# A decoder layer on one core: the 512×4096×1024 W_down product by seven block products in place of eight

## The chip, the cores and the metric

The kernel runs on one core of a Trainium2 chip. The metric is the device time of one execution in microseconds (us); less is better. Three executions of the kernel before were timed, and one more was recorded by the hardware profiler. Five engines work side by side: PE (TensorE, matrix products; its weight loads are listed as PEld), DVE (VectorE), ACT (ScalarE), POOL (GpSimd) and SP (SyncE, which issues the DMA transfers here). Each takes its own instructions in order and waits on semaphores for the others.

## The reference

One layer for 512 tokens of width 1024, all in f32. Cut to what matters:

```
h = rms_norm(x, g_pre_mix);  proj = h @ w_in
q, k, v, cb, cc, cu, ga, gc = split(proj)
y_attn = stick_breaking_attention(q, k, v) @ w_attn_out      # 8 heads x 64
y_conv = (cb * causal_dwconv3(cc * cu)) @ w_conv_out
mixed = (sigmoid(ga) * y_attn + sigmoid(gc) * y_conv) @ w_o
x = x + rms_norm(mixed, g_post_mix)
f = relu(rms_norm(x, g_pre_mlp) @ w_up)**2 @ w_down          # 1024 -> 4096 -> 1024
x = x + rms_norm(f, g_post_mlp)
x = x + sigmoid(rms_norm(x, g_ple) @ w_ple_gate) * (p @ w_ple_proj)
```

## The kernel before

Every large product is made with three matmuls: each f32 operand is **split** into a high part (an ACT cast to the type fp32r) and a low part (a DVE subtraction of the high part from the source), and high×high, high×low and low×high are added up in PSUM (`mm3`, lines 82 to 85; `split`, lines 60 to 62). So each weight matrix is loaded as f32 into one of four `raw` buffers, cast by ACT, subtracted by DVE, and only then read by PE. Weights that come in columns (`wcols`) or rows (`wrow`) are split in two halves of 128x512; the split pair lies in `wlo` and `whi`, five buffers each.

The stages stand in this order: head (norm of x, transposes, v), attention and convolution, **mix** (line 408: for each of 8 column blocks two gate products and one product with W_attn_out and W_conv_out), **W_o** (`rows`, line 489), the small p @ W_ple_proj (line 493), **up** (lines 512 to 532: 32 column blocks of W_up, each 24 matmuls of 512 columns, followed by `relu2`, which leaves the activations in eight f32 tiles `af`, 8 KB a partition), **W_down** (line 562) and the **gate product** with W_ple_gate (line 567 on).

`rows` runs k outermost over the row blocks of a weight, for all four token blocks t and both halves of the columns, into eight PSUM banks; the last four k are kept back and run token block by token block, and after each the chain of norm, residual and next norm starts (`residual`, `chain1`, `chain2`), whose result is transposed on PE two token blocks later (`transposed2`). For W_down that is 32 row blocks × 4 token blocks × 2 column halves × 3 = 768 matmuls of 512 columns. In each chain, `rstd_of` ends with a 128x1 power on POOL (line 119); this and the masks of the attention are all that POOL computes.

PE and SP issue in the order in which the code stands (`manual_schedule`, line 35). The order on ACT, DVE and POOL is made by the framework's scheduler when the kernel is built. A buffer is given out again when the last reader of its former content is done; the writer waits for that. SP's queue is one line: a transfer that waits for its buffer holds back all the transfers behind it.

Of the kernel before, what the change touches and what calls it, by code (L numbers as in the profile page):

```python
# [8 lines left out]
F32 = mybir.dt.float32  # L9
# [14 lines left out]
FF = 4096  # L24
EPS = 1e-6
# [6 lines left out]
def hybrid_block(ctx, tc, x, p, g_pre_mix, w_in, b_gate, w_conv, w_attn_out, w_conv_out, w_o,  # L32
# [10 lines left out]
    wts = ctx.enter_context(tc.tile_pool(name="wts", bufs=5))  # L43
# [5 lines left out]
    psp = ctx.enter_context(tc.tile_pool(name="psp", bufs=8, space=bass.MemoryType.PSUM))  # L49

# [13 lines left out]
    def weights(loads, shape):  # L64
        raw = raws.tile(shape, F32, tag="raw", name="raw")
        for sel, src in loads(raw):
            nc.sync.dma_start(sel, src)
        lo = wts.tile(shape, F32R, tag="wlo", name="wlo")
        hi = wts.tile(shape, F32R, tag="whi", name="whi")
# [3 lines left out]
        return hi, lo  # L73

# [7 lines left out]
    def mm3(ps, lh, ll, rh, rl, start, stop):  # L82
        nc.tensor.matmul(ps, lh, rh, start=start, stop=False)  # L83
        nc.tensor.matmul(ps, lh, rl, start=False, stop=False)  # L84
        nc.tensor.matmul(ps, ll, rh, start=False, stop=stop)  # L85
# [322 lines left out]
    for j in range(NK):  # L408
        sa, sc = sg if j == 0 else (gate(j, 0), gate(j, 1))
# [27 lines left out]
    def rows(nk, stat, w, tail, chain):  # L437
        acc = {}
        held = {}
        for k in range(nk):  # L440
            wk = wrow(w, k)
            if k >= nk - tail:
                held[k] = wk
                continue
            sh, sl = stat(k)
            for t in range(NT):
                tok = slice(t * P, (t + 1) * P)
                for hf in range(2):
                    if k == 0:
                        acc[t, hf] = bank()  # L450
                    cs = slice(hf * 512, (hf + 1) * 512)
                    mm3(acc[t, hf], sh[:, tok], sl[:, tok], wk[0][:, cs], wk[1][:, cs], k == 0, False)
        for t in range(NT):
# [7 lines left out]
            chain(t, [acc[t, 0], acc[t, 1]])  # L461

# [52 lines left out]
    for half in range(2):  # L515
        ns = slice(half * 256, (half + 1) * 256)
        for c in range(2):
# [8 lines left out]
            if half == 1:  # L526
                relu2(c, ups[c])
    for c in range(2, FF // P):
        if c == 8:
            gpl = gain(g_post_mlp)  # L530
            gle = gain(g_ple)
        relu2(c, proj(wcols(w_up, c * P), hm))

    a_s = {}
    pgw = {}

    def acts(c):
        g = c // 4
        if g not in a_s:
            a_s[g] = (bigt([P, 4, S], name="ah"), bigt([P, 4, S], name="al"))  # L540
            for i in range(4):
                split(a_s[g][0][:, i], a_s[g][1][:, i], af[g][:, i])
            if 4 <= g < 7:
                i = g - 4
                wl = bigt([P, 2, D], name="pgl")
                wh = bigt([P, 2, D], name="pgh")
                for kk in range(2):
                    pgw[2 * i + kk] = (wh[:, kk], wl[:, kk])
                    raw = raws.tile([P, D], F32, tag="raw", name="raw")
                    nc.sync.dma_start(raw, w_pg[(2 * i + kk) * P:(2 * i + kk + 1) * P, :])  # L550
                    split(wh[:, kk], wl[:, kk], raw)
        return a_s[g][0][:, c % 4], a_s[g][1][:, c % 4]

    hn2 = {}
    h3 = hpair("h3")

    def chain2(t, accs):
        hn2[t] = residual(xr[t // 2][:, t % 2, :], accs, gpl, gle)
        if t > 1:
            transposed2(h3, hn2[t - 2], t - 2)  # L560

    rows(FF // P, acts, w_down, 4, chain2)
    for k in range(6, NK):
        pgw[k] = wrow(w_pg, k)

# [1 line left out]
    for t in range(NT):  # L567
        if t == 1:
            transposed2(h3, hn2[3], 3)
        tok = slice(t * P, (t + 1) * P)  # L570
        for cs in CUTS[t]:
            n = cs.stop - cs.start
            ps = bank()[:, 0:n]
            for k in range(NK):
                mm3(ps, h3[0][k // 4][:, k % 4, tok], h3[1][k // 4][:, k % 4, tok],
                    pgw[k][0][:, cs], pgw[k][1][:, cs], k == 0, k == NK - 1)
            if t == 0 and cs.start == 0:
                transposed2(h3, hn2[2], 2)
            sg = tm()[:, 0:n]
            nc.scalar.activation(sg, ps, AF.Sigmoid)  # L580
# [31 lines left out]
```

## Time and profile before

| | before |
|---|---|
| median of 3 timed runs (lowest to highest) | 768.4 us (766.04 to 769.82) |
| the profiled execution: first to last instruction | 764.4 us |
| median of the timed runs above that span | 4.0 us |
| W_down, first to last matmul | about 538 to 713 us of the span |
| up | about 364 to 538 us |
| gate product, to the last output | about 713 to 764 us |
| granted PE clock, mean | 1.000 |
| mean rate of all DMA transfers | 102 GB/s |

The time of the profiled execution itself is not listed beside its span, so the span is set against the median of the timed runs. A row of the groups reads: line, engine, operation, written tile <- read tiles, shape, number; then the busy time of all, the mean of one in ns, and how long the engine had stood idle before them, with what ended most of that. A row of the windows gives for each engine the busy time and the number of instructions that fall into the stretch.

### The profile page before, as it was taken

To read this page: it belongs to the slowest core of one execution; us is meant where nothing else is said; L and a number is where in the kernel's file an instruction comes from. 1 tells how busy PE (TensorE), PEld (TensorE's weight loads), DVE (VectorE), ACT (ScalarE), POOL (GpSimd) and SP (SyncE) were. 2 spreads that over 40 slices of the span, in tenths; PEclk is the share of its full clock that TensorE was granted. 3 is DMA by queue.
4 is the path that set the end of the run, shared out by engine and by line. 5 is a ranking of instruction groups with operands and counts; after the bars stand their busy time and mean duration, and the time that the engine had idled before them with its cause. 6 is when DMAs were issued, how large, how long until landed. Compare 5 with 4: busy or idle time off the path is not lost.

```text
span 764.4 us, 9131 instructions
## 1 busy us (share of the span) xinstructions
PE 756.4 (99%) x3528; PEld 631.9 (83%) x3528; DVE 388.1 (51%) x643; ACT 301.7 (39%) x586; POOL 49.8 (7%) x91
## 2 busy tenths in 40 slices
PE   8999999999999999999999999999999999999997
PEld 6888888888888888888988888888888888888886
DVE  5759797976434345348433333333652543234742
ACT  7654645554333334228323232323631433222511
POOL 1013314040000000001000000000000000000100
PEclk9999999999999999999999999999999999999999
DMA  9512130414634623211633333332323442410011
GB/s 303 163 58 83 55 111 29 131 31 115 193 111 130 200 87 106 83 56 34 187 86 108 86 107 89 104 101 94 110 84 109 138 165 87 161 56 1 0 56 55
DMA packets 91106, 77.66 MB, mean 102 GB/s; under 512 B 2580, under 2 KB 81208, under 8 KB 91064
## 3 DMA queue, kind: packets, MB, share of 16 engines
q1 hardware_dynamic: 91064, 77.10, 32.9%
q8 instruction: 27, 0.44, 0.2%
q14 instruction: 15, 0.12, 0.1%
HBM read 74.99 MB, written 2.10 MB: 101 GB/s over the span
## 4 chain that ended last, share of the span: by engine, by line
PE 98%; ACT 1%; DMA 1%; DVE 0%; issue 0%; SPq 0%; POOL 0%; ACTq 0%
PE ps L83 31%; PE ps L85 31%; PE ps L84 31%; PE ps L334 1%; PE ps L320 1%; PE ps L127 1%; PE ps L293 1%; PE ps L292 1%; DMA xin<-in_x_dram 1%; ACT h1h L197 0%; PE ps L188 0%; ACT vh L61 0%; ACT junk L111 0%; PE ps L433 0%; POOL rs L119 0%
## 5 line engine op out<-in xcount | busy, mean ns | idle before, releaser
L62 DVE TENSOR_TENSOR wlo<-raw,whi 128x512 fp32r<-128x512 f32 x236 | 158.2, 686 | 253.2 <-ACT whi L61 253.0
L61 ACT CAST whi<-raw 128x512 fp32r<-128x512 f32 x236 | 141.5, 623 | 328.1 <-PE ps L84 174.8
L83 PE MATMUL ps<-h1h,whi 128*128 128x512 f32 x288 | 113.0, 392 | 0.0
L85 PE MATMUL ps<-h1h,wlo 128*128 128x512 f32 x288 | 112.3, 390 | 0.0
L84 PE MATMUL ps<-h1l,whi 128*128 128x512 f32 x288 | 112.2, 390 | 0.0
L83 PE MATMUL ps<-h2h,whi 128*128 128x512 f32 (+1 forms) x272 | 102.5, 377 | 0.0
L84 PE MATMUL ps<-h2l,whi 128*128 128x512 f32 (+1 forms) x272 | 102.4, 377 | 0.0
L85 PE MATMUL ps<-h2h,wlo 128*128 128x512 f32 (+1 forms) x272 | 102.4, 377 | 0.0
L83 PE MATMUL ps<-whi,ah 128*128 128x512 f32 x256 | 99.7, 389 | 0.0
L85 PE MATMUL ps<-whi,al 128*128 128x512 f32 x256 | 99.6, 389 | 0.0
L84 PE MATMUL ps<-wlo,ah 128*128 128x512 f32 x256 | 99.6, 389 | 0.0
L85 PEld LDWEIGHTS ps<-h1h,wlo 128*128 128x128 f32 x288 | 54.1, 188 | 11.2
L84 PEld LDWEIGHTS ps<-h1l,whi 128*128 128x128 f32 x288 | 54.1, 188 | 10.9
L83 PEld LDWEIGHTS ps<-h1h,whi 128*128 128x128 f32 x288 | 54.1, 188 | 10.8
L85 PEld LDWEIGHTS ps<-h2h,wlo 128*128 128x128 f32 x272 | 51.2, 188 | 9.4
L84 PEld LDWEIGHTS ps<-h2l,whi 128*128 128x128 f32 x272 | 51.2, 188 | 9.4
L83 PEld LDWEIGHTS ps<-h2h,whi 128*128 128x128 f32 x272 | 51.2, 188 | 9.3
L84 PEld LDWEIGHTS ps<-wlo,ah 128*128 128x128 f32 x256 | 48.1, 188 | 10.0
L85 PEld LDWEIGHTS ps<-whi,al 128*128 128x128 f32 x256 | 48.1, 188 | 9.9
L83 PEld LDWEIGHTS ps<-whi,ah 128*128 128x128 f32 x256 | 48.1, 188 | 9.9
L119 POOL TENSOR_TENSOR rs<-ms,mhalf 128x1 f32<-128x1 f32 x20 | 11.8, 588 | 565.7 <-DVE ms L117 513.5
L301 POOL TENSOR_SCALAR_AFFINE_SELECT beta<-beta 128x128 f32<-128x128 f32 x32 | 26.3, 833 | 107.9 <-ACT beta L295 107.7
(133 smaller groups left out, 1000.3 us busy)
## 6 DMA issues: line engine op xcount, KB each, us to landing
raw<-in_w_in_dram SPq DMA_DIRECT2D x36, 512.0 KB, 3.8
raw<-in_w_up_dram SPq DMA_DIRECT2D x32, 512.0 KB, 4.0
raw<-in_w_down_dram SPq DMA_DIRECT2D x32, 512.0 KB, 3.3
raw<-in_w_o_dram SPq DMA_DIRECT2D x8, 512.0 KB, 3.4
raw<-in_w_ple_gate_dram SPq DMA_DIRECT2D x8, 512.0 KB, 3.3
xin<-in_x_dram SPq DMA_DIRECT2D x4, 512.0 KB, 9.5
vr<-in_w_in_dram SPq DMA_DIRECT2D x4, 512.0 KB, 7.5
raw<-in_w_conv_out_dram SPq DMA_DIRECT2D x8, 256.0 KB, 2.8
```

The lines of the kernel that those rows point to most:

```text
L61: nc.scalar.copy(hi, src)
L62: nc.vector.tensor_tensor(lo, src, hi.bitcast(F32), op=ALU.subtract)
L83: nc.tensor.matmul(ps, lh, rh, start=start, stop=False)
L84: nc.tensor.matmul(ps, lh, rl, start=False, stop=False)
L85: nc.tensor.matmul(ps, ll, rh, start=False, stop=stop)
L119: nc.gpsimd.tensor_tensor(r, m, mhalf, op=ALU.pow)
L127: nc.tensor.transpose(ps[:, i * P:(i + 1) * P], hn[g][:, i * P:(i + 1) * P], ident)
L292: nc.tensor.matmul(ps[:, c0:c0 + n], lhs, st[:, 1, 0:n], start=True, stop=False)
L293: nc.tensor.matmul(ps[:, c0:c0 + n], lhs, st[:, 2, 0:n], start=False, stop=True)
L301: nc.gpsimd.affine_select(t_[:, dg], t_[:, dg], pattern=[[-1, P]], compare_op=ALU.is_gt, fill=fill, base=0, channel_multiplier=1)
L320: nc.tensor.transpose(ps[:, c0 + (qb - kb) * P:c0 + (qb - kb + 1) * P], w[:, o:o + P], ident)
L334: nc.tensor.matmul(ps[:, kb * P:S], lhs, wt[i][:, c0:c0 + n], start=(kb == 0 and i == 0), stop=(kb == NT - 1 and i == 1))
```

## The change

The W_down product is cut into 2×2 blocks: the tokens into 0 to 255 and 256 to 511, the 4096 inner columns into two halves (16 row blocks of 128 each), and the 1024 output columns into two halves. Seven products of such blocks, taken of sums and differences of blocks (Strassen's method in Winograd's form), replace eight.

- **Sums of the weight** (`make_sums`, `save_sums`): for each of the 16 row blocks j of a half, SP loads the rows j of both halves (two transfers of 512 KB), POOL makes four differences of 128x512, and SP later writes them to a DRAM scratch tile (two transfers). One such step stands before the gates of mix blocks 2 to 7, one at the start and one behind W_o, and one at every third column block of up from 3 to 24. The stores stand in SP's line behind later weight loads.
- **Sums of the activations**: DVE, in place in `af`: four additions during up (behind the column blocks 19, 23, 27 and 31) and twelve subtractions of 128x4x256 during the first three products.
- **The seven products** run one after the other in the order 1, 2, 6, 7, 5, 3, 4, each as 8 weight tiles of 128x2x512 (`load_t`, from W_down or from the scratch) against 4 groups of activations of 128x4x256 (`load_s`), for two token blocks; each weight tile serves 12 matmuls. Each tile and each group is split anew for each product. At the end of a product ACT or DVE takes the two accumulators into f32 tiles `cx`; products 6, 5 and 4 go on adding into the banks of 1, 6 and 7.
- **Pools**: the ten weight buffers become one ring of 13 (`wts`), which also holds the inputs and outputs of the sums and later `cx`.
- **End**: the chains of token blocks 0 and 1 stand behind product 3 and inside product 4; the gate product takes token blocks 0 and 1 first, in two halves of k, then 2 and 3. In mix, the first gate of block 1 stands between the two halves of block 0's output products.

```diff
-    wts = ctx.enter_context(tc.tile_pool(name="wts", bufs=5))
+    wts = ctx.enter_context(tc.tile_pool(name="wts", bufs=13))
...
+    def make_sums():
+        save_sums()
+        j = next(made)
+        q = []
+        for h in range(2):
+            t = w4()
+            nc.sync.dma_start(t, wd[j][h].rearrange("p (c n) -> p c n", c=2))
+            q += [t[:, 0], t[:, 1]]
+        dst = wsum[j // 2][:, :, j % 2, :]
+        o = [w4(), w4()]
+        t1, t2, t3, t4 = (o[i // 2][:, i % 2] for i in range(4))
+        for r, x_, y_ in ((t1, q[1], q[0]), (t2, q[3], t1), (t3, q[3], q[1]), (t4, q[2], t2)):
+            nc.gpsimd.tensor_tensor(r, x_, y_, op=ALU.subtract)
+        unsaved.extend([(dst[:, 0:2], o[0]), (dst[:, 2:4], o[1])])
...
     for c in range(2, FF // P):
...
+        if c % 3 == 0 and c < 27:
+            make_sums()
+        if c % 3 == 2:
+            save_sums()
         relu2(c, proj(wcols(w_up, c * P), hm))
+        if c > 16 and c % 4 == 3:
+            g = c // 4 - 4
+            nc.vector.tensor_tensor(quarter(1, 0, g), quarter(1, 0, g), quarter(1, 1, g), op=ALU.add)
...
+    ORDER = (1, 2, 6, 7, 5, 3, 4)
...
+    def load_t(n, i):
+        raw = raws.tile([P, 2, 512], F32, tag="raw", name="raw")
...
+        nc.sync.dma_start(raw, src)
+        lo, hi = w4(F32R), w4(F32R)
+        split(hi, lo, raw)
...
+    def load_s(n, g):
...
+        split(hi, lo, quarter(*LEFT[n], g))
...
+        if n == 1:
+            nc.vector.tensor_tensor(a11, quarter(1, 0, g), a11, op=ALU.subtract)
+        elif n == 2:
+            nc.vector.tensor_tensor(a12, a12, a11, op=ALU.subtract)
+        elif n == 6:
+            nc.vector.tensor_tensor(a11, quarter(1, 1, g), a11, op=ALU.subtract)
...
-    rows(FF // P, acts, w_down, 4, chain2)
-    for k in range(6, NK):
-        pgw[k] = wrow(w_pg, k)
...
+    AFTER = {(3, 7): lambda: chain2(0), (4, 1): lambda: chain2(1), (4, 2): lambda: load_pg(0),
+             (4, 4): lambda: load_pg(2), (4, 5): lambda: turn(0)}
+    nt = ns = 0
+    for n, i in plan_t:
+        while ns < min(len(plan_s), plan_s.index((n, i // 2)) + 3):
+            load_s(*plan_s[ns])
+            ns += 1
+        while nt < min(len(plan_t), plan_t.index((n, i)) + 4):
+            load_t(*plan_t[nt])
+            nt += 1
+        for t in range(2):
...
+            for j in (2 * i, 2 * i + 1):
+                sh, sl = stat[n, j]
+                th, tl = tiles[n, j]
+                mm3(acc[n, t], sh[:, ts], sl[:, ts], th, tl, j == 0 and n in (1, 2, 7, 3),
+                    j == NJ - 1, n in (6, 5, 4))
+            if i == NI - 1:
+                done(n, t)
+        if (n, i) in AFTER:
+            AFTER[n, i]()
+    turn(1)
+    for t in range(2, NT):
+        chain2(t)
+        for k in range(2 * t, 2 * t + 2):
+            pgw[k] = wrow(w_pg, k)
...
+    top = [(t, cs, bank()) for t in range(2) for cs in CUTS[0]]
+    for half in range(2):
+        for t in range(2):
+            for k in range(4 * half, 4 * half + 4):
+                for t_, cs, ps in top[2 * t:2 * t + 2]:
+                    pg_mm(ps, t, cs, k)
+            if (half, t) == (1, 1):
+                turn(2)
...
+    turn(3)
```

What this does to the order on three engines. **POOL, in the chains behind W_o** (`rs` is the 128x1 power of a chain, two for each token block; the `w_` tiles are the inputs and outputs of one step of sums; L294 is the subtraction in `make_sums`). Before, behind the last masks of the attention (L301), all powers of these chains and of those behind W_down follow each other:

```order
L301 AFFINE_SELECT beta<-beta 128x128 x2
L301 AFFINE_SELECT keep<-keep 128x128 x2
L301 AFFINE_SELECT beta<-beta 128x128
L301 AFFINE_SELECT keep<-keep 128x128
L119 TENSOR_TENSOR rs<-ms,mhalf 128x1 x16
```

and now:

```order
L294 TENSOR_TENSOR w_3196<-w_3193,w_3195 128x512
L124 TENSOR_TENSOR rs<-ms,mhalf 128x1 x7
L294 TENSOR_TENSOR w_3465<-w_3461 128x512
L294 TENSOR_TENSOR w_3465<-w_3463,w_3465 128x512
L294 TENSOR_TENSOR w_3466<-w_3463,w_3461 128x512
L294 TENSOR_TENSOR w_3466<-w_3463,w_3465 128x512
L124 TENSOR_TENSOR rs<-ms,mhalf 128x1
```

One whole step of sums stands between the seventh and the eighth power, that is inside the chain of token block 3.

**DVE, where up ends and W_down begins.** Before (L510 is `relu2`, `al` the low part of an activation, `wlo` of a weight):

```order
L510 SCALAR_TENSOR_TENSOR af<-ps,tmp 128x512
L62 TENSOR_TENSOR wlo<-raw,whi 128x512
L62 TENSOR_TENSOR al<-af,ah 128x512 x7
L62 TENSOR_TENSOR wlo<-raw,whi 128x512 x2
L62 TENSOR_TENSOR al<-af,ah 128x512
```

and now, from the low parts of the second and third group of product 1 on (`sb`; they take buffers that are free only when up's last matmul is done). L632 and L593 are sums of activations, L560 is `relu2` of the last column block, `w_4662`, `w_4684` and `w_4702` are the low parts of the weight tiles 4, 5 and 6 of product 1:

```order
L64 TENSOR_TENSOR sb<-af,sb 128x1024 x2
L632 TENSOR_TENSOR af<-af 128x4x256
L560 SCALAR_TENSOR_TENSOR af<-ps,tmp 128x512
L632 TENSOR_TENSOR af<-af 128x4x256
L593 TENSOR_TENSOR af<-af 128x4x256
L64 TENSOR_TENSOR w_4662<-raw,w_4663 128x1024
L64 TENSOR_TENSOR sb<-af,sb 128x1024
L64 TENSOR_TENSOR w_4684<-raw,w_4685 128x1024
L632 TENSOR_TENSOR af<-af 128x4x256
L64 TENSOR_TENSOR w_4702<-raw,w_4703 128x1024
```

Between the weight tiles stand the splits of the groups and the sums of activations.

**SP, in up.** Before, the weights of the column blocks follow each other, with two gain vectors (`gb`) behind the eighth:

```order
L67 DMA raw<-in_w_o_dram 128x1024 x8
L67 DMA raw<-in_w_up_dram 128x8x128 x8
L104 DMA gb<-in_g_post_mlp_dram 128x1024
L104 DMA gb<-in_g_ple_dram 128x1024
L67 DMA raw<-in_w_up_dram 128x8x128 x24
```

and now, for three column blocks (L288 loads the inputs of one step of sums, L278 stores its outputs):

```order
L288 DMA w_3705<-in_w_down_dram 128x1024
L288 DMA w_3707<-in_w_down_dram 128x1024
L69 DMA raw<-in_w_up_dram 128x8x128 x2
L278 DMA wsum_415<-w_3709 128x2x512
L278 DMA wsum_415<-w_3710 128x2x512
L69 DMA raw<-in_w_up_dram 128x8x128
```

Every third weight load stands behind two stores that wait for POOL.

More of the change, by code (lines that the diff above doesn't have):

```diff
@@ L263, in hybrid_block, with save_sums @@
     hx = mov(h1)
+    wd = w_down.rearrange("(h j p) n -> j h p n", h=2, p=P)
+    wsum = [sums.tile([P, 4, 2, 512], F32, name=f"wsum{i}") for i in range(NJ // 2)]
+    unsaved = []
+    def save_sums():
+        while unsaved:
+            dst, src = unsaved.pop(0)
+            nc.sync.dma_start(dst, src)
+    made = iter(range(NJ))
+    def make_sums():
[12 more added lines that the diff above has]
+        unsaved.extend([(dst[:, 0:2], o[0]), (dst[:, 2:4], o[1])])
     def proj_q(j):
@@ L531, in hybrid_block @@
             gle = gain(g_ple)
+        if c % 3 == 0 and c < 27:
+            make_sums()
+        if c % 3 == 2:
+            save_sums()
         relu2(c, proj(wcols(w_up, c * P), hm))
-    a_s = {}
-    pgw = {}
[L537 to L552, printed above, removed]
@@ new lines, in load_s @@
+    def load_s(n, g):
+        if (n, g) == (1, 0):
+            hi, lo = (wts.tile([P, 4, 256], F32R, tag="w", name="s0") for _ in range(2))
+        else:
+            both = bigt([P, 2, 4, 256], name="sb")
+            hi, lo = both[:, 0], both[:, 1]
+        split(hi, lo, quarter(*LEFT[n], g))
+        for v in range(4):
+            stat[n, 4 * g + v] = hi[:, v], lo[:, v]
+        a11, a12 = quarter(0, 0, g), quarter(0, 1, g)
+        if n == 1:
[4 more added lines that the diff above has]
+            nc.vector.tensor_tensor(a11, quarter(1, 1, g), a11, op=ALU.subtract)
@@ new lines, in hybrid_block, with load_pg, turn @@
+    pgw = {}
+    def load_pg(k):
+        wl, wh = bigt([P, 2, D], name="pgl"), bigt([P, 2, D], name="pgh")
+        for kk in range(2):
+            pgw[k + kk] = (wh[:, kk], wl[:, kk])
+            raw = raws.tile([P, D], F32, tag="raw", name="raw")
+            nc.sync.dma_start(raw, w_pg[(k + kk) * P:(k + kk + 1) * P, :])
+            split(wh[:, kk], wl[:, kk], raw)
+    def turn(t):
+        if not h3:
+            h3.extend(hpair("h3"))
+        transposed2(h3, hn2[t], t)
+    plan_t = [(n, i) for n in ORDER for i in range(NI)]
@@ new lines, in hybrid_block @@
+    top = [(t, cs, bank()) for t in range(2) for cs in CUTS[0]]
[6 more added lines that the diff above has]
+                turn(2)
+            if (half, t) == (1, 0):
+                for args in top[:2]:
+                    gated(*args)
+    turn(3)
+    for args in top[2:]:
+        gated(*args)
@@ L571, in hybrid_block @@
+    for t in range(2, NT):
         for cs in CUTS[t]:
-            n = cs.stop - cs.start
-            ps = bank()[:, 0:n]
+            ps = bank()[:, 0:cs.stop - cs.start]
             for k in range(NK):
[L575 to L580, printed above, removed]
```

103 lines of the change are left out of this document (83 added, 20 removed).

## The prediction

> **What bounds the kernel now.** I read the page first, then the waits of PE, then PE's instructions in order of time within W_down.
>
> ```profile
> span 764.4 us, 9131 instructions
> PE 756.4 (99%) x3528; PEld 631.9 (83%) x3528; DVE 388.1 (51%) x643; ACT 301.7 (39%) x586; POOL 49.8 (7%) x91
> PE 98%; ACT 1%; DMA 1%; DVE 0%; issue 0%; SPq 0%; POOL 0%; ACTq 0%
> ...
> PE ps L169 <- POOL ident masks.py:199: 1.4, 1, 1.4
> PE ps L84 <- DVE vl L62: 1.0, 1, 1.0
> PE ps L83 <- ACT vh L61: 1.0, 1, 1.0
> PE ps L188 <- DVE xin L178: 0.2, 1, 0.2
> ```
>
> A busy PE is not yet PE at its peak, but here three views agree: PE is busy 99% of the span, the chain that ended last is PE for 98%, and PE waited for others 3.6 us in all (line, releaser, total us, times, longest), every bit of it in the head. So time falls only where PE issues less, and rises only where something new makes PE wait. The question is how fast the stream of matmuls is.
>
> ```profile
> 544.81 0.39 PE L84 MATMUL ps<-wlo,ah 128*128 128x512 f32 x1
> ...
> 548.89 0.39 PE L84 MATMUL ps<-wlo,ah 128*128 128x512 f32 x1
> ```
>
> These are the first and the last of 19 matmuls in a row, start and modelled length first: 18 steps in 4.08 us, so **0.2267 us** each. The 0.39 us is latency, not the price.
>
> **What is removed.** W_down has 32 row blocks × 4 token blocks × 2 halves × 3 = 768 matmuls of 512 columns. Seven products have 7 × 16 row blocks × 2 token blocks × 3 = 672, of the same shape. 96 × 0.2267 = **21.8 us** less on PE. All other stages keep their matmuls. This is the whole gain; the rest of the working asks what PE must now wait for.
>
> **W_down on DVE and ACT.** The new splits are 56 weight tiles and 28 groups, each 1024 wide, and 12 sums of activations of that size.
>
> ```profile
> L62 DVE TENSOR_TENSOR pgl<-raw,pgh 128x1024 fp32r<-128x1024 f32 x6 | 7.3, 1224 | 19.6 <-ACT pgh L61 16.3 <-PE ps L84 3.3
> L61 ACT CAST pgh<-raw 128x1024 fp32r<-128x1024 f32 x6 | 6.3, 1050 | 18.4 <-DMA raw<-in_w_ple_gate_dram 18.4
> L510 DVE SCALAR_TENSOR_TENSOR af<-ps,tmp 128x512 f32<-128x512 f32 x32 | 21.8, 683 | 0.0
> 538.00:713.00 175.00, 175.00 (x778) 145.04 (x777) 72.97 (x115) 62.44 (x113) 2.75 (x5) 1.00 0.30 97
> ```
>
> The last row is the window of W_down: its length, then busy time of PE, PEld, DVE, ACT and POOL, the granted clock, the DMA share and GB/s. DVE was busy 73 of 175 us. Now a group of activations lasts PE 24 matmuls, 5.44 us, in which DVE makes two weight tiles, one group and, in products 1, 2 and 6, one sum: 4 × 1.224 = 4.90 us, or 90%. In the other four products it is 3 × 1.224 = 3.67 us. ACT needs 3 × 1.05 = 3.15 us. Both fit, and the f32 sums, which the trace doesn't show, are taken at 1.224 as the nearest row of that size; at half of it DVE has 80%, at 1.5 times it 101%, which would cost PE 12 × 0.08 us, about 1 us. The buffers let DVE run three to four weight tiles ahead, 8 to 11 us.
>
> The tightest place is the seam. Groups two and three of product 1 need buffers that up holds to its last matmul. Counted from there, the DVE rows shown with the change make tile 4 after one cast and six steps of 1.224 and one of 0.683: 1.05 + 7.34 + 0.68 = 9.1 us. PE reaches tile 4 after four tiles of 12 matmuls, 10.9 us. Tile 5 is ready at 11.5 (wanted at 13.6), tile 6 at 14.0 (16.3). It fits by 1.8 us: cost **0**, with up to 3 us if hand-overs take more.
>
> **The sums on POOL.** Sixteen steps of four subtractions 128x512, two inputs each.
>
> ```profile
> L301 POOL TENSOR_SCALAR_AFFINE_SELECT beta<-beta 128x128 f32<-128x128 f32 x32 | 26.3, 833 | 107.9 <-ACT beta L295 107.7
> L301 POOL TENSOR_SCALAR_AFFINE_SELECT keep<-keep 128x128 f32<-128x128 f32 x32 | 12.6, 404 | 0.8 <-ACT keep L296 0.8
> L119 POOL TENSOR_TENSOR rs<-ms,mhalf 128x1 f32<-128x1 f32 x20 | 11.8, 588 | 565.7 <-DVE ms L117 513.5 <-DVE ms L115 52.2
> raw<-in_w_up_dram SPq DMA_DIRECT2D x32, 512.0 KB, 4.0
> 184.00:305.00 121.00, 121.00 (x540) 100.29 (x539) 52.17 (x77) 40.51 (x69) 0.00 (x0) 1.00 0.43 135
> 364.00:538.00 174.00, 174.00 (x814) 146.04 (x814) 62.98 (x101) 53.91 (x100) 0.00 (x0) 1.00 0.35 106
> ```
>
> No such operation is in the trace. From below it costs 0.59 us (the 128x1 power), from above 4 × 0.833 = 3.3 us. I take 4 × 0.404 = **1.6 us**, from the mask that doesn't wait for another engine. A step then takes 6.4 us, and one comes every three column blocks, 3 × 24 × 0.2267 = 16.3 us. POOL was idle in mix and up (the two windows, mix first), and DVE busy 43% and 36% of them, so POOL's work stands beside PE's. A step's second input waits until PE has left the column block five before; the two weight loads behind it are thus 5 × 5.44 = 27 us early, and the third stands behind POOL and its own 4.0 us of landing and is still some 20 us early (38 less 4 less 6.4 less 4 less the split). In SP's line nothing reaches PE late: cost 0. New traffic is 1 MB in and 1 MB out in 16.3 us, 129 GB/s on top of the windows' 106 to 135, and about 193 GB/s in W_down (512 KB for 12 matmuls); the head's first slice moved 303, so I count nothing.
>
> [...]
>
> ```profile
> 355.52 0.93 POOL L119 TENSOR_TENSOR rs<-ms,mhalf 128x1 f32<-128x1 f32 x1 [2.19 <-DVE ms L117]
> 361.03 0.55 POOL L119 TENSOR_TENSOR rs<-ms,mhalf 128x1 f32<-128x1 f32 x1 [4.58 <-DVE ms L115]
> 361.62 1.41 DVE L475 SCALAR_TENSOR_TENSOR tmp<-xr,rs,gb 128x512 f32<-128x512 f32 x2
> 365.73 1.04 PE L127 MATMUL ps<-ident,tmp 128*128 128x128 f32 x8
> L469 DVE TENSOR_TENSOR xr<-xr,tmp 128x512 f32<-128x512 f32 x16 | 10.3, 683 | 0.0
> ```
>
> Only here does a step stand in a chain that PE waits for: between the seventh and the eighth power behind W_o. Its inputs wait for W_o's last matmuls and land before 355. It would run from 356.5 to 356.5 + 6.4 = 362.9, so the eighth power is 1.9 us late; two residual additions that may change places with it add 1.4. PE wants the result 2.7 us after it was ready (363.0 against 365.7). So 3.3 − 2.7 = **0.6 us**; nothing at 0.59 us a subtraction, 7 us at 3.3.
>
> **The end.** In product 4 (21.8 us and 0.9 us of transposes) DVE has to make five weight tiles and four gate tiles (9 × 1.224 = 11.0), two whole chains (each two 128x1024 products and an addition, twice the 128x512 rows: 1.41 + 1.37 + 1.41 = 4.2) and two or three small steps (2 us): 21.4 of 22.7 us until PE transposes token block 1. I charge **1 us** for a fit that close. Chains 2 and 3 lie under the 96 matmuls of the upper token blocks. The last transposes are followed at once by the matmuls that need them; before, 1.74 us of two such rounds had other matmuls behind them. Two sigmoids, a cast and a subtraction must pass:
>
> ```profile
> L580 ACT ACTIVATE tmp<-ps 128x512 f32<-128x512 f32 (+1 forms) x9 | 5.0, 552 | 29.9 <-PE ps L85 29.9
> L61 ACT CAST h3h<-ps 128x512 fp32r<-128x512 f32 x8 | 4.4, 588 | 0.0
> L62 DVE TENSOR_TENSOR h3l<-ps,h3h 128x512 fp32r<-128x512 f32 x8 | 5.4, 682 | 0.0
> ```
>
> 2 × 0.55 + 0.59 + 0.68 = 2.4 us, less 1.74: **0.7 us**. The first gate of mix block 1, put between two products, gains nothing, as PE didn't wait there.
>
> **Sum.** 764.4 − 21.8 + 0.6 + 1.0 + 0.7 = 744.9 us of span. The timed runs' median of 768.4 lies 4.0 above the span; kept, that gives **748.9 us**. With all bounds at their good ends it is 746.6, with all at their bad ends (1 + 3 at the seam, 7, 3 and 2 at the end) 762.6.
>
> **Rivals.**
> - *DVE runs dry in W_down.* For it: 90% of three products, 21.4 of 22.7 us at the end, and every tile needs a cast first. Against it: four products at 67% and a lead of 8 to 11 us. If each of the 96 steps of 1024 cost 0.1 us more in hand-overs, products 1, 2 and 6 would miss their pace by nothing (5.3 of 5.44) but the seam and the end would lose about 1 and 3 us; at 0.3 us more the twelve groups with sums lose 0.66 us each, 8 us, and the two places 4 to 6: some **760 us**.
> - *POOL sets the pace of mix and up*, through SP's line: the next inputs stand behind the stores, the stores behind POOL. A round is 4.0 us of landing and four subtractions; it outlasts PE's 16.3 us from 3.1 us a subtraction on. With 14 rounds and 27 us of lead, the saving is gone at 4 × T = 12.3 + (27 + 21.8) / 14, T = 3.95 us. [...] For it: no such row in the trace. Against it: 4 × 0.404.
> - *The saving doesn't show*: the many tiles, each with its own waits, slow the stream. At 672 matmuls 0.032 us more for each eats the 21.8 us: **768 us**. Against it: every weight of before brings PE a wait for its high and its low part too, and PE's 3.6 us of waiting all lie in the head.
>
> [...]
>
> **Chances.** Forecast 0.68, DVE dry 0.17, POOL's pace 0.06, no saving shown 0.05, something else 0.04, a quarter of it slower than before. The range of 8 in 10 reaches from the best sum, less the spread of the timed runs (about 2 us), into the first rival: **744.8 to 760**. Within 0.5% of 768.4, about what a measurement of this kernel can tell from no change, lie 764.6 to 772.2: faster 0.88, the same 0.05, slower 0.07.
>
> **What would show it.** Right: 672 matmuls in W_down at 0.227 us, PE busy 98% or more, waits of PE beyond the head of 1 to 5 us in all, found behind W_o and at the two ends of product 4. DVE dry: PE waits for low parts `w` at L64 through products 1, 2 and 6. POOL's pace: PE waits for weights in up, and a subtraction's row above 3 us. Wrong altogether: a step other than 0.227 us, or a granted clock below 1.00.

## The result and the profile after

| | before | changed |
|---|---|---|
| median of 4 runs on one chip (lowest to highest) | 768.58 us (766.04 to 769.82) | 746.85 us (745.09 to 748.66) |
| ratio, 95% interval | | 0.9727 [0.9701, 0.9752] |
| profiled execution: span | 764.4 us | 746.9 us |

The forecast was 748.9 us, with a range of 744.8 to 760.0. The page of the changed kernel has nearly the shape of that of before: PE is busy for 99% of the span, and PE makes up 93% of the chain that ended last (98% before; the chain now runs through the powers and additions behind W_o as well).

```profile
PE 737.6 (99%) x3432; PEld 616.6 (83%) x3432; DVE 461.5 (62%) x645; ACT 339.6 (45%) x576; POOL 136.2 (18%) x155
...
PE 93%; DVE 2%; POOL 1%; issue 1%; ACT 1%; DMA 1%; SPq 0%; ACTq 0%; POOLq 0%
```

POOL's busy time has risen to 136.2 us and DVE stands at 62%, yet the waits of PE (line, releaser, total us, times, longest) hold only one entry from behind the head, the 0.2 us for `h2l` behind W_o:

```profile
PE ps L88 <- ACT vh L63: 1.8, 1, 1.8
PE ps L174 <- POOL ident masks.py:199: 1.4, 1, 1.4
PE ps L89 <- DVE vl L64: 1.1, 1, 1.1
PE ps L89 <- DVE h2l L64: 0.2, 1, 0.2
PE ps L193 <- DVE xin L183: 0.2, 1, 0.2
```

The matmuls of W_down follow each other as before. Here are the first and the last of 17 in product 6, start and modelled length first:

```profile
599.67 0.39 PE L89 MATMUL ps<-w,sb 128*128 128x512 f32 x1
...
603.30 0.39 PE L90 MATMUL ps<-w,sb 128*128 128x512 f32 x1
```

16 steps in 3.63 us are 0.2269 us each, against 0.2267 before; the two agree within the rounding of the starts.

Where the time went is read from the tile rows of PE. Each gives the number of matmuls on a tile and the start of the first and of the last one: `oyh` begins mix, `mh` W_o, `pt` the small product, `h2h` up, `h3h` the gate product. First before, then the changed kernel:

```profile
L83 PE MATMUL ps<-oyh,whi x64: 389/389/447, 184.9 to 303.9; 128*128 128x512 f32 x64
L83 PE MATMUL ps<-h2h,whi x272: 277/389/396, 362.9 to 537.8; 128*128 128x512 f32 x120, 128*128 128x256 f32 x16
L83 PE MATMUL ps<-pgh,h3h x54: 278/389/476, 714.2 to 758.9; 128*128 128x512 f32 x42, 128*128 128x256 f32 x12
```

```profile
L88 PE MATMUL ps<-oyh,whi x64: 389/389/447, 188.3 to 307.4; 128*128 128x512 f32 x64
L88 PE MATMUL ps<-h2h,whi x272: 277/389/396, 366.3 to 541.6; 128*128 128x512 f32 x120, 128*128 128x256 f32 x16
L88 PE MATMUL ps<-pgh,h3h x36: 278/389/476, 696.3 to 740.4; 128*128 128x512 f32 x28, 128*128 128x256 f32 x8
```

Mix begins 3.4 us later in the changed kernel's profile, although PE has the same work ahead of it; what differs there is the granted clock, as is shown below. From its begin to the end of the span it takes 558.6 us against 579.5: **20.9 us less**. From the last row of up to the gate product it is 154.7 against 176.4, 21.7 us less, which is the whole of the 96 matmuls (21.8). Up itself takes 0.4 us more (175.3 against 174.9), the gate product with the end 0.4 us more (50.6 against 50.2). The table does the same for every kernel that was run: differences of these starts, in us. The medians come from several chips: beside the experiments, before had 767.02, 768.43 and 767.88 us.

| kernel | head, to mix | mix | W_o | small product | up and W_down | gate product to the end | median of the runs |
|---|---|---|---|---|---|---|---|
| before | 184.9 | 120.5 | 45.3 | 12.2 | 351.3 | 50.2 | 768.58 |
| changed | 188.3 | 120.6 | 45.3 | 12.1 | 330.0 | 50.6 | 746.85 |
| eight plain products | 184.5 | 120.6 | 45.3 | 12.3 | 351.4 | 50.2 | 768.27 |
| later steps | 185.7 | 120.6 | 45.3 | 12.2 | 329.6 | 50.5 | 745.96 |
| sums on DVE | 187.2 | 120.6 | 45.3 | 12.0 | 331.8 | 50.2 | 751.12 |
| lower tokens first | 184.3 | 120.6 | 45.3 | 12.0 | 343.3 | 54.0 | 763.45 |
| double sums on DVE | 187.7 | 120.6 | 45.3 | 12.0 | 329.9 | 50.6 | 748.44 |
| two of three matmuls | 185.5 | 120.6 | 45.3 | 12.0 | 298.2 | 52.1 | 717.59 |
| POOL ×1.5 | 187.2 | 120.6 | 45.3 | 14.4 | 332.4 | 50.6 | 750.42 |
| POOL ×2 | 186.1 | 120.7 | 59.0 | 16.1 | 334.9 | 50.6 | 768.12 |
| POOL ×3 | 187.6 | 150.1 | 65.3 | 13.7 | 381.4 | 50.3 | 850.18 |
| POOL ×2, inputs first | 188.1 | 120.6 | 45.3 | 15.7 | 329.6 | 50.5 | 749.94 |
| POOL ×2, both | 187.2 | 120.5 | 45.4 | 12.2 | 329.6 | 50.7 | 746.68 |

Two things are to be seen here. The head lasts 184.3 to 188.3 us with the same work in it, so a difference of 2 or 3 us between two medians can be the head alone; the stages behind it repeat to 0.1 to 0.3 us where nothing was changed, the end to 0.5. And the columns say at once in which stage a kernel pays.

The traces show what sets the head. Here are 10 us of it, before and then changed (length, then busy time and number of PE, PEld, DVE, ACT and POOL, then the granted clock, the DMA share and GB/s):

```profile
8.00:18.00 10.00, 8.05 (x36) 6.03 (x37) 8.97 (x25) 9.02 (x26) 1.10 (x2) 1.00 1.10 356
```

```profile
8.00:18.00 10.00, 7.11 (x23) 5.57 (x22) 7.73 (x21) 8.60 (x25) 0.55 (x1) 0.66 1.09 359
```

In the changed kernel's profile the granted clock is 0.50 for 6.8 us, from about 10.7 to 17.5 us, and 1.00 again from there on; half of 6.8 is the 3.4 us. The pages of all 13 kernels give the clock by fortieths of the span: the four with the longest heads (changed, double sums on DVE, POOL ×3, and POOL ×2 with the inputs first: 187.6 to 188.3 us) have 0.8 in the first one, the other nine (184.3 to 187.2) 0.9 or more. It varies within one kernel too: the four timed runs of the changed kernel list mean granted clocks of 0.994 to 1.000. What starts such a stretch is not shown.

### The profile page after: what moved, and what is told of

The parts are those of the page before. It is cut to its first block, busy times and chain, and to the rows that moved or that the text cites. A ratio compares the mean times of both kernels' runs of the same rounds, so it can differ in the third digit from the quotient of the medians.

```text
span 746.9 us, 9291 instructions
## 1 busy us (share of the span) xinstructions
PE 737.6 (99%) x3432; PEld 616.6 (83%) x3432; DVE 461.5 (62%) x645; ACT 339.6 (45%) x576; POOL 136.2 (18%) x155
## 4 chain that ended last, share of the span: by engine, by line
PE 93%; DVE 2%; POOL 1%; issue 1%; ACT 1%; DMA 1%; SPq 0%; ACTq 0%; POOLq 0%
PE ps L89 29%; PE ps L90 29%; PE ps L88 29%; PE ps L366 1%; PE ps L352 1%; POOL w L294 1%; DMA xin<-in_x_dram 1%; PE ps L325 1%; PE ps L324 1%; POOL rs L124 1%; DVE tmp L517 1%; PE ps L132 0%; PE ps L193 0%; DVE xr L518 0%; DVE tmp L524 0%
## 5 line engine op out<-in xcount | busy, mean ns | idle before, releaser
L64 DVE TENSOR_TENSOR wlo<-raw,whi 128x512 fp32r<-128x512 f32 x176 | 128.0, 761 | 112.9 <-ACT whi L63 45.8
L63 ACT CAST whi<-raw 128x512 fp32r<-128x512 f32 x176 | 101.8, 626 | 85.9 <-PE ps L90 44.2
L64 DVE TENSOR_TENSOR w<-raw,w 128x1024 fp32r<-128x1024 f32 x56 | 68.3, 1220 | 36.1 <-PE ps L89 18.3
L88 PE MATMUL ps<-w,sb 128*128 128x512 f32 x216 | 84.1, 389 | 0.0
L90 PE MATMUL ps<-w,sb 128*128 128x512 f32 x216 | 84.0, 389 | 0.0
L89 PE MATMUL ps<-w,sb 128*128 128x512 f32 x216 | 84.0, 389 | 0.0
L63 ACT CAST w<-raw 128x1024 fp32r<-128x1024 f32 x56 | 58.4, 1052 | 30.1 <-PE ps L90 21.5
L294 POOL TENSOR_TENSOR w<-w,w 128x512 f32<-128x512 f32 x48 | 62.2, 1315 | 32.4 <-DMA w<-in_w_down_dram 25.2
L124 POOL TENSOR_TENSOR rs<-ms,mhalf 128x1 f32<-128x1 f32 x20 | 14.3, 717 | 266.8 <-DVE ms L120 257.9
L88 PEld LDWEIGHTS ps<-h1h,whi 128*128 128x128 f32 x288 | 54.1, 188 | 10.7
L559 ACT ACTIVATE tmp<-ps 128x512 f32<-128x512 f32 x32 | 19.1, 598 | 89.1 <-PE ps L90 89.0
```

Of the source, the lines that this page charges most:

```text
L63: nc.scalar.copy(hi, src)
L64: nc.vector.tensor_tensor(lo, src, hi.bitcast(F32), op=ALU.subtract)
L88: nc.tensor.matmul(ps, lh, rh, start=start, stop=False, skip_group_check=onto)
L89: nc.tensor.matmul(ps, lh, rl, start=False, stop=False, skip_group_check=onto)
L90: nc.tensor.matmul(ps, ll, rh, start=False, stop=stop, skip_group_check=onto)
L124: nc.gpsimd.tensor_tensor(r, m, mhalf, op=ALU.pow)
```

## The experiments

**Theory.** The time is the number of matmuls times 0.2267 us, and all the new work of POOL, DVE and the DMAs lies under it. The rivals: the gain comes from the new staging; DVE is nearly the bound; POOL sets a pace.

### Is it the count?

Eight plain block products in the new staging. The sums of the weight and of the activations are left out:

```diff
-    ORDER = (1, 2, 6, 7, 5, 3, 4)
...
+    ORDER = tuple(range(8))
+    LEFT = {n: (n // 4, n % 2) for n in ORDER}
+    RIGHT = {n: (n % 2, n // 2 % 2) for n in ORDER}
...
```

> Eight plain block products of W_down in the new staging: same tiles, same splits on DVE and ACT, same order at the end, but no sums of W_down on GpSimd, no sums of activations, 768 matmuls in place of 672. Count theory (only the number of matmuls at 0.2267 us decides): 96 x 0.2267 = 21.8 us above the changed kernel's 746.9, that is 768.6, between 766 and 771, about the kernel of before. Rival (the new staging and the new end of the kernel bring the gain, not the seven products): 752 or less. Rival (the sums cost PE time in other stages): clearly below 766.

Measured: 768.27 us, ratio to before 1.0009 [0.9991, 1.0026].

```profile
PE 756.2 (99%) x3528; PEld 631.6 (83%) x3528; DVE 439.5 (58%) x633; ACT 348.6 (46%) x588; POOL 51.1 (7%) x91
```

PE has 96 matmuls more than in the changed kernel, and the stretch from up to the gate product takes 351.4 − 330.0 = 21.4 us more. The staging, the tiles, the split for each product and the new end bring nothing by themselves; they cost nothing either. The seven products are the gain.

### The step of sums behind W_o

In the changed kernel four subtractions stand between two powers of the chain behind W_o. POOL and DVE, from the timeline (start, us):

```profile
358.35 0.55 POOL L124 TENSOR_TENSOR rs<-ms,mhalf 128x1 f32<-128x1 f32 x1 [1.60 <-DVE ms L122]
358.87 1.29 POOL L294 TENSOR_TENSOR w<-w 128x512 f32<-128x512 f32 x1
360.24 4.81 POOL L294 TENSOR_TENSOR w<-w,w 128x512 f32<-128x512 f32 x3
365.01 0.54 POOL L124 TENSOR_TENSOR rs<-ms,mhalf 128x1 f32<-128x1 f32 x1
```

```profile
353.03 1.28 DVE L518 TENSOR_TENSOR xr<-xr,tmp 128x512 f32<-128x512 f32 x2
...
360.26 2.38 DVE L518 TENSOR_TENSOR xr<-xr,tmp 128x512 f32<-128x512 f32 x2
```

The same two additions on DVE take 1.28 us while POOL is quiet and 2.38 while it subtracts; POOL's three subtractions take 4.81, 1.60 each, against 1.31 on average. Both are slower here, DVE by 1.1 us and POOL by 0.29 us a subtraction; whether that had a part in the cost of the step is not shown. The edit takes the step out of that place and starts the steps of up later:

```diff
-    make_sums()
     pp = [bigt([P, 2, D], F32, "pp") for _ in range(2)]
...
-        if c % 3 == 0 and c < 27:
+        if c % 3 == 2 and c > 4:
             make_sums()
-        if c % 3 == 2:
+        if c % 3 == 1:
             save_sums()
```

> The step of sums behind W_o is left out there and the steps of up start two column blocks later, so that no subtraction stands between the seventh and the eighth power behind W_o; the same 16 steps in all. Theory (the step in the chain costs 0.4 us there): PE's wait of 0.2 us for the low part of the normed block is gone, and from the end of mix to the first W_down matmul PE takes 0.3 to 0.5 us less; the time 746.5, not told apart from 746.9 by the clock. Rival (those 0.4 us come from elsewhere in up): the stretch keeps its length. Rival (later steps reach W_down too late): PE waits for sums in products 5 to 4, 748 or more.

Measured: 745.96 us (745.28 to 746.99). The waits of PE are those of the head alone:

```profile
PE ps L174 <- POOL ident masks.py:199: 1.4, 1, 1.4
PE ps L88 <- ACT vh L63: 1.0, 1, 1.0
PE ps L89 <- DVE vl L64: 0.7, 1, 0.7
```

The stretch of up and W_down is 329.6 against 330.0, and all of it lies in up: 174.9 us, as in before, against 175.3. So the step cost 0.4 us there. Behind the head no form with all 672 matmuls is faster, but its runs cannot be told apart from those of the changed kernel.

### Did the sums have to be on POOL?

```diff
-            nc.gpsimd.tensor_tensor(r, x_, y_, op=ALU.subtract)
+            nc.vector.tensor_tensor(r, x_, y_, op=ALU.subtract)
```

> The 64 subtractions of W_down blocks on DVE in place of GpSimd. If nothing but the matmul count decides and DVE has room in mix, W_o and up: 745 to 749, and the 128x512 split on DVE, 761 ns on average with GpSimd at work, falls back to the 686 to 690 ns of before; behind W_o the step of four subtractions stands in DVE's own chain and may cost 0 to 3 us. If contention between DVE and GpSimd costs PE time, the time falls by over 1 us. If GpSimd was needed because DVE is too full: 752 or more.

Measured: 751.12 us (748.76 to 751.69), between the two expectations. The split and the subtraction in the groups, and the two waits that are new, in the profile of this run:

```profile
L64 DVE TENSOR_TENSOR wlo<-raw,whi 128x512 fp32r<-128x512 f32 x176 | 115.0, 685 | 62.3 <-PE ps L89 26.3 <-issue 16.6 <-DMA wsum<-w 9.8
L294 DVE TENSOR_TENSOR w<-w,w 128x512 f32<-128x512 f32 x48 | 31.7, 688 | 40.8 <-DMA w<-in_w_down_dram 24.5 <-PE ps L89 16.3
...
PE ps L88 <- ACT h2h L63: 1.2, 1, 1.2
PE ps L89 <- DVE h2l L64: 0.5, 1, 0.5
```

The groups of the changed kernel have 761 ns for the same split and 1315 ns for a subtraction:

```profile
L64 DVE TENSOR_TENSOR wlo<-raw,whi 128x512 fp32r<-128x512 f32 x176 | 128.0, 761 | 112.9 <-ACT whi L63 45.8 <-PE ps L89 22.7 <-issue 20.0
L294 POOL TENSOR_TENSOR w<-w,w 128x512 f32<-128x512 f32 x48 | 62.2, 1315 | 32.4 <-DMA w<-in_w_down_dram 25.2 <-PE ps L89 7.2
```

So a subtraction takes DVE half of what it takes POOL, and POOL's work adds 176 × 0.076 = 13 us to DVE's splits, all of it hidden. With the sums on DVE both waits stand behind W_o, where the subtractions queue in DVE's chain, and up and W_down take 1.8 us more. The profiled run was the fastest of the four; the others took 2 to 3 us more and list a mean granted clock of 0.993 against its 0.996. Over 750 us that is some 2 us of clock; no trace here shows in which stage. DVE was not too full (no wait of PE in the rest of up, or in W_down).

### The gate product's order

```diff
-    top = [(t, cs, bank()) for t in range(2) for cs in CUTS[0]]
...
+    turn(2)
+    for t in (2, 3, 0, 1):
+        if t == 3:
+            turn(3)
+        for cs in CUTS[3 if t == 1 else 0]:
```

> The gate product takes token blocks 2, 3, 0, 1 in place of 0, 1, 2, 3. Block 2's normed rows are ready at 707.6 us of the changed kernel's span, PE is through with W_down and its transposes at 695.7. Theory (the order upper tokens first hides chains 2 and 3): PE waits some 12 us for block 2 and, with transposes and splits in the open, 1 to 2 more; block 3 is ready at 714.3 and then hidden under block 2's matmuls: 759 to 761. Rival (the chains would start as early whatever the order and something else hides them): within 2 us of 746.9.

Measured: 763.45 us (761.21 to 765.3), above the expectation; the profiled run took 761.21.

```profile
PE ps L132 <- DVE ms L120: 11.3, 1, 11.3
...
PE ps L90 <- DVE h3l L64: 0.9, 1, 0.9
```

With a third one of 0.3 us for `h3h` the waits are 12.5 us, as expected, and the gate product begins 13.3 us later (343.3 against 330.0). But it also lasts 3.4 us longer. The windows behind the pause, in the same form as those of the head, show why:

```profile
705.00:712.00 7.00, 6.14 (x17) 4.30 (x17) 4.48 (x6) 2.15 (x4) 0.55 (x1) 0.55 0.00 0
712.00:719.00 7.00, 7.00 (x33) 5.79 (x32) 1.38 (x2) 0.60 (x1) 0.00 (x0) 1.00 0.11 40
```

After the pause PE had a clock of 0.55 and made 17 instructions where it makes 33. A wait of 11 us so cost 11 us and some 3 more, which the expectation did not have.

### How much room had DVE?

Each sum of activations is followed by a second operation of its shape that changes nothing:

```diff
+        for a, m in ((a11, 1), (a12, 2), (a11, 6)):
+            if n == m:
+                nc.vector.tensor_tensor(a, a, a, op=ALU.max)
```

> Each of the 12 sums of activations in products 1, 2 and 6 is followed by a second operation of the same shape on DVE that changes nothing (the maximum of a tile with itself): 12 x 1.22 us more DVE work, 6.1 us for every 5.44 us of matmuls in these products in place of 4.9. Theory (DVE at 90% is covered, with a lead of some 8 us): the 12 x 0.68 = 8.2 us are mostly eaten by the lead, 747 to 751. Rival (DVE is already on the path in these products): 12 x 1.22 = 14.6 us more, 760 or more. Rival (DVE has far more room than the sum says): no wait of PE in W_down at all, 746 to 747.5.

Measured: 748.44 us (747.85 to 748.72); up and W_down take 329.9 us, as in the changed kernel, and PE has no wait in W_down. Behind the head the profiled run takes 558.4 us, the changed kernel 558.6; all four of its runs list a granted clock of 0.994 or 0.995, which can account for the 1.6 us between the medians. The median lies in the range of the theory, but what the trace shows is the rival with far more room: no wait at all. Product 6 in the windows, first the changed kernel, then this one (DVE is the third busy time):

```profile
585.80:607.60 21.80, 21.80 (x97) 18.03 (x97) 15.10 (x14) 10.84 (x11) 0.00 (x0) 1.00 0.63 194
```

```profile
585.00:606.80 21.80, 21.80 (x97) 17.92 (x96) 21.80 (x21) 12.01 (x12) 0.00 (x0) 1.00 0.55 172
```

DVE is full there now and still keeps up, because its operations follow each other faster than their listed length:

```profile
596.11 1.22 DVE L64 TENSOR_TENSOR sb<-af,sb 128x1024 fp32r<-128x1024 f32 x1
597.24 1.22 DVE L64 TENSOR_TENSOR w<-raw,w 128x1024 fp32r<-128x1024 f32 x1
598.38 1.22 DVE L636 TENSOR_TENSOR af<-af 128x1024 f32<-128x1024 f32 x1
```

1.135 us from start to start: the four of a group take 4.54 of 5.44 us, five take 5.67, and 12 × 0.23 = 2.8 us is less than the lead.

To see the other end, the high×low matmul of every three was left out of W_down:

```diff
-                mm3(acc[n, t], sh[:, ts], sl[:, ts], th, tl, j == 0 and n in (1, 2, 7, 3),
...
+                nc.tensor.matmul(acc[n, t], sh[:, ts], th, start=j == 0 and n in (1, 2, 7, 3), stop=False,
+                                 skip_group_check=onto)
+                nc.tensor.matmul(acc[n, t], sl[:, ts], th, start=False, stop=j == NJ - 1, skip_group_check=onto)
```

> The high by low matmul of every three is left out in the W_down products (the output is less exact): 448 matmuls there in place of 672, all DVE and ACT work unchanged. If PE alone sets the time: 224 x 0.2267 = 50.8 us less, 696. Theory (DVE becomes the bound at once): a group lasts PE 3.63 us and DVE 4.9 in products 1, 2 and 6, 12 x 1.27 = 15 us less a lead of some 8, and product 4 with its chains is 6 us late: 696 + 13 to 21, 709 to 717, with PE's waits at the low parts of tiles and groups. If the step of the matmul itself changed, the rows would show another distance than 0.2267 us.

Measured: 717.59 us, two runs (715.48 and 719.7), 0.6 above the upper end. Up and W_down take 298.2 us, 31.8 less and not 50.8; 19 us are lost again. PE's waits in W_down and behind it:

```profile
PE ps L701 <- ACT w L63: 5.7, 11, 1.6
PE ps L132 <- DVE ms L120: 3.2, 1, 3.2
PE ps L132 <- DVE w L509: 3.1, 1, 3.1
```

These are 12 us: weight tiles that come late in eleven places, and two chains at the end. The granted clock, 0.992 on average over the span of 713.7 us (5.7 us of it, head and end included), can hold a part of the rest, which isn't in the list. PE's listed waits at the tiles are for ACT's casts, and not for the low parts that were expected; but DVE is busy for 116.8 of the 122.9 us of this W_down, and ACT for 87.8. So with a third of PE's work taken away DVE and the chains are the bound at once, as the theory said. In the changed kernel the splits are covered by PE's own length, and a faster matmul would bring less than its share (here 31.8 of 50.8 us).

### POOL's pace

First every subtraction twice, then three times:

```diff
+            for _ in range(2):
-            nc.gpsimd.tensor_tensor(r, x_, y_, op=ALU.subtract)
+                nc.gpsimd.tensor_tensor(r, x_, y_, op=ALU.subtract)
```

> Every subtraction on GpSimd is done twice, the second time with the same result: 2 x 1.32 = 2.6 us a subtraction, 10.5 us a step. Theory: a round of 4.0 + 10.5 = 14.5 us stays below PE's 16.3 us of three column blocks, so the pace of mix and up costs nothing, and only the chain behind W_o pays: 5.3 us more between the seventh and the eighth power, 746.9 + 5 = 752 (750 to 754), with a wait of some 5 us for the normed block. Rival (the pace of GpSimd, or its blocking of DVE, already reaches PE): over 756, with waits for weights in up.

> Every subtraction on GpSimd is done three times: 3.95 us a subtraction, 15.8 us a step, the value at which the prediction's formula had the saving gone. By that formula (14 rounds in one line, each 4.0 + 15.8 = 19.8 us against 16.3, less 27 us of lead): 22 us more, about 769, and with the chain behind W_o (10.5 us more) up to 779. Rival (W_o lets GpSimd catch up, so that the lead counts twice, and a step's own landing overlaps the step before): the pace costs 0 to 5 us in all and the chain 10.5: 757 to 763.

Measured: 768.12 us (ratio to before 0.9994 [0.9977, 1.0011]) and 850.18 us (1.1057 [1.1024, 1.109]). **Both theories fell**, and of the rivals only the doubled form's "over 756" held, though its waits do not lie where it put them: twice the work on POOL eats the whole saving, three times loses 82 us on top. In the table, the doubled form pays 13.7 us in W_o, 4.0 in the small product and 4.9 in up; the tripled form 29.5 in mix, 20.0 in W_o and 51.4 in up. (W_o pays in the doubled form for mix: the last step ahead of W_o begins on POOL at 294.8 us, at 281.3 in the changed kernel. The weights of W_o wait for buffers of the same ring, ACT's first casts 7.2 us for POOL, and five of their loads stand in SP's line behind the stores of that step. Of the 13.7 us PE stands idle for 8.0; the rest goes with the granted clock: from 313 to 325 us the matmuls that follow each other come 0.43 us apart, and the page has 0.6 in the slice from 307 to 326 us.) Here is POOL in up: the changed kernel, then twice, then three times.

```profile
439.21 1.30 POOL L294 TENSOR_TENSOR w<-w 128x512 f32<-128x512 f32 x1 [8.55 <-PE ps L90]
...
455.53 1.30 POOL L294 TENSOR_TENSOR w<-w 128x512 f32<-128x512 f32 x1 [8.55 <-PE ps L90]
```

```profile
451.84 3.10 POOL L295 TENSOR_TENSOR w<-w 128x512 f32<-128x512 f32 x2 [7.23 <-DVE wlo L64]
455.02 7.65 POOL L295 TENSOR_TENSOR w<-w,w 128x512 f32<-128x512 f32 x6
470.20 3.10 POOL L295 TENSOR_TENSOR w<-w 128x512 f32<-128x512 f32 x2 [7.53 <-DVE wlo L64]
```

```profile
512.20 4.05 POOL L295 TENSOR_TENSOR w<-w 128x512 f32<-128x512 f32 x3 [7.45 <-DVE wlo L64]
...
535.62 4.29 POOL L295 TENSOR_TENSOR w<-w 128x512 f32<-128x512 f32 x3 [7.90 <-DMA w<-in_w_down_dram]
```

In the changed kernel a round takes 16.32 us and POOL waits for PE. With more on POOL a round takes 18.4 and 23.4 us here, and POOL still stands idle for 7.2 to 7.9 us of each: a round is POOL's work **plus** some 7.5 us. The prediction had 4.0 us there, the landing of one transfer. In SP's line, though, the second store waits for POOL's last subtraction, a weight load stands behind it, and the next step's two inputs behind that: 2 MB that can only start when POOL has ended, and in the doubled form the inputs land 6.4 us after their issue. One run was to show that the loop begins at a level (six subtractions in place of four), two that the line makes it.

```diff
+            for _ in range(2 if y_ is q[1] and x_ is q[3] or y_ is t2 else 1):
-            nc.gpsimd.tensor_tensor(r, x_, y_, op=ALU.subtract)
+                nc.gpsimd.tensor_tensor(r, x_, y_, op=ALU.subtract)
```

> Two of the four subtractions of a step are done twice: six of 1.31 us, 7.9 us a step in place of 5.3. Theory after the two runs before (a round lasts what GpSimd computes plus some 7.4 us in which the saves, one weight load and the next inputs pass SP's line and land): 7.9 + 7.4 = 15.3 us, below PE's 16.3 in up, so up keeps its length and only the chain behind W_o pays some 2.6 us: 749 to 751. Rival (every microsecond on GpSimd costs PE in proportion, as between the kernel and its doubled form: 21 us for 84): 757 to 758.

Measured: 750.42 us (748.78 to 752.22). Where POOL catches up with PE in up, its rounds last 14.9 and 15.6 us (7.9 + 7.4), so they fit. The small product and up pay 2.3 and 2.4 us, where the chain from W_o reaches them, together more than the 2.6 that were expected; up's share is mostly waits for `h2h` and `h2l` before 377 us. So there is a level, and not a price by the microsecond.

In the next run each step asks for its inputs before it stores the sums of the step before (POOL's work stays doubled):

```diff
     def make_sums():
-        save_sums()
         j = next(made)
...
             q += [t[:, 0], t[:, 1]]
+        save_sums()
...
         wo2 = weights(two, [P, NK, P])
-        save_sums()
...
-        if c % 3 == 2:
+        if c == 26:
             save_sums()
```

> Every subtraction on GpSimd twice, as in the doubled run (768.1), but a step's inputs are asked for ahead of the saves of the step before, in SP's line. Theory (the 7.4 us between one step's last subtraction and the next one's first are the line: saves, a weight load, then inputs): GpSimd goes on without the gap, a round is 10.5 us and fits into 16.3; the chain behind W_o stays 5 us longer: 751 to 755. Rival (GpSimd and DVE keep each other out, or the DMA engines are full): 765 or more.

Measured: 749.94 us (748.63 to 751.55) in place of 768.12, with the same 128 subtractions.

```profile
447.63 2.66 POOL L295 TENSOR_TENSOR w<-w 128x512 f32<-128x512 f32 x2 [4.25 <-PE ps L90]
451.49 8.10 POOL L295 TENSOR_TENSOR w<-w,w 128x512 f32<-128x512 f32 x6 [1.21 <-DMA w<-in_w_down_dram]
463.95 2.66 POOL L295 TENSOR_TENSOR w<-w 128x512 f32<-128x512 f32 x2 [4.36 <-PE ps L90]
```

A round is 16.32 us again and POOL waits for PE. The place of the stores in SP's queue was worth 18 us. What is left, 3.6 us in the small product, is the chain behind W_o (1.5 us of waits; a part of the rest can be the granted clock, 0.993 on average against 0.998 in the next run); the last run moves that step too, as above.

> As the run with the inputs first, every subtraction twice, and in addition no step between the powers behind W_o (steps of up two column blocks later). If the line and that chain are all that a doubled GpSimd costs: 746 to 749, as the changed kernel itself. If GpSimd's work slows DVE or the DMAs in other places as well: 752 or more.

Measured: 746.68 us (745.9 to 747.35), as the changed kernel, with double the work on POOL. Its splits on DVE are the slowest of all runs, and nothing waits for them:

```profile
L64 DVE TENSOR_TENSOR wlo<-raw,whi 128x512 fp32r<-128x512 f32 x176 | 146.9, 870 | 73.2 <-ACT whi L63 33.6 <-PE ps L89 14.5 <-issue 12.7
```

## Why the prediction was right, point by point

- **The bound and the gain.** Right: 21.8 us were forecast for W_down, 21.7 were found, and eight products in the same staging give them back.
- **The seam and DVE in W_down, cost 0.** Right, and with more room than was said: tile 4's low part was done at 548.2 us, some 5 us before PE came to it, where 1.8 were forecast. DVE began the two splits of the seam at 540.7, 1.4 us before up's last matmul and not behind it, and 1.224 us was taken for an operation's price, while its step is 1.135. The reading that was applied to the matmuls (0.39 us listed, 0.2267 from start to start) was left out for DVE.
- **The step behind W_o, 0.6 us.** Right in size, 0.4 us measured, and right that the step costs it; the way there was another, so the size is partly luck. A subtraction takes 1.31 us on average, but in this place, beside DVE's additions, the step of four took 6.2 us (358.87 to 365.05), about the 6.4 of the sum with 1.6 each. It began at once behind the seventh power, so the eighth was 0.6 us late and not 1.9 (365.01 less the 3.4 us by which the head is longer, against 361.03); the additions, 1.1 us slower, were done before POOL was free and did not add to that. The transposes, where the sum had PE wait, began without a wait, 2.1 us after their input was ready. PE lost its 0.4 us behind them, at the low part `h2l`, which DVE made only at 372.6 us, behind six splits of weights.
- **The end, 1.0 and 0.7 us.** Mis-sized: 0.4 in all, and the same end takes 50.2 to 50.7 us in the other kernels, so even the 0.4 is hardly clear of the spread. Before the transposes of token block 1 PE had no wait; DVE's 21.4 us of work there was counted at listed lengths. At the last transposes the sigmoids did not stand in the way; the 16 of them take 1.66 us, and the matmul that needs them follows at once:

```profile
718.00 0.39 PE L90 MATMUL ps<-whi,h3l 128*128 128x512 f32 x1
718.23 1.91 PE L132 MATMUL ps<-ident,w 128*128 128x128 f32 x16
719.89 0.48 PE L88 MATMUL ps<-pgh,h3h 128*128 128x512 f32 x1
```

- **The 4.0 us above the span.** In each run of a changed form the time is 1.7 to 1.8 us above its own span (748.66 and 746.9; 766.01 and 764.3 of the eight products), in those of before 1.7 to 2.9. So before's span of 764.4 belonged to a run at the short end, some 766 to 767 us, and the rest of the 4.0 was its short head, without half clock. Taking it over unchanged did no harm, since the changed kernel's head varies in the same way.
- **The sum.** 768.58 less 20.9 is 747.7. The forecast was 748.9: the end and the chain, 2.3 us, came to 0.8, and the rest is the spread of the head.
- **POOL's pace, the second rival.** Its mechanism was named rightly and its price was wrong. The step that failed is "a round is 4.0 us of landing and four subtractions; it outlasts PE's 16.3 us from 3.1 us a subtraction on", with 27 us of lead. The idle part of a round is 7.5 us, so it outlasts PE's 16.3 from (16.3 − 7.5) / 4 = 2.2 us on, and the lead is small: 8 rounds of 7.1 us too much should have cost 57 us in up in the tripled form, and cost 51, which leaves some 6 us of lead in place of 27. The saving was to be gone at 3.95 us a subtraction; it was gone at 2.6, and at 3.95 the time was 850 and not 769. The chance of 0.06 was thus too low for what was known: the bounds of a subtraction were 0.59 to 3.3 us, and the upper one, which was priced at 7 us in the range, would have cost some 60 (an estimate, on a straight line between the doubled form's 21 at 2.6 us and the tripled one's 103 at 3.95). The sum also had no term for the clock: behind the head the doubled form loses 22.6 us, and PE waits in only 13.1 of them; its mean granted clock is 0.983, 13 us of its span of 767.4, head and end included. The forecast held because a subtraction takes 1.31 us, which no row of before showed.
- **The saving not shown.** Ruled out by the step of 0.2269 us in W_down.
- **The signs.** PE is busy for 99% (98 or more was named), and it issues 96 matmuls less than with the eight products, at the old step. Waits of 1 to 5 us beyond the head were forecast; the list has 0.2 and the stages 0.8, so this sign was missed on the good side. A granted clock below 1.00 was named as a sign of being wrong altogether, and the profiled run has a mean of 0.994. While PE had work, that is the 6.8 us at half clock in the head alone: from about 17.5 us to the last matmul the clock is 1.00. So the change did not bring it, and the sign was drawn too sharply.

## What to carry to other kernels

In this kernel, where PE is busy for 99% of the span, matmuls that were not issued were time saved one to one (96 of them, 21.7 us), as long as each engine that works beside it kept its own pace; a pace is the work of a round plus everything that stands between the end of one round and the start of the next, and in a queue that is one line that includes the stores, the loads behind them and their landing (some 7.5 us here). Ask for the next round's inputs ahead of the last round's stores (18 us here, with POOL's work doubled). And where an operation's price is known only by bounds, work the loop out once more at the upper bound: a lead counted in buffers is soon used up (27 us were counted here, some 6 found).

## What the hardware showed that was not expected

- While PE waited for 11.3 us (lower tokens first) its granted clock fell to 0.50, and stayed there from about 697.6 to 711.3 us (0.74 in the window from 691 to 705 us, 0.55 from 705 to 712); the matmuls came at 0.43 us instead of 0.227. Full speed came back 7.6 us after PE had begun again (703.67), with a wait of 0.9 us in between. The 13.7 us are twice the 6.8 in the changed kernel's head; what sets such a length is not shown.
- DVE's and POOL's instructions take longer where both are at work, without any wait that the profile lists: the 128x512 split takes 685 ns with POOL free of sums and 761 with 64 subtractions. Their number alone does not set it: with 128 it takes 799 ns where POOL waits in SP's line, and 867 or 870 where the inputs come first; POOL's own subtractions then rise from 1313 to 1459 and 1474 ns. That the two engines meet more often there is argued, not shown; nor does a trace show that one keeps the other out, as two of the rivals had it.
- The head with the same work takes 184.3 to 188.3 us. In the kernel of before (184.9 us) the granted clock is 1.00 from 9 to 18 us of the span; in the changed one (188.3 us) it is 0.50 for 6.8 us of them.
